# Layer 1's gate and branch products: weights as the moving operand, 512 features at a time

## The chip, the cores and the metric

The kernel runs on one core of a Trainium2 chip. The metric is device time in microseconds (us) of one execution; lower is better.

## What is computed

The reference is a backbone of two layers over 256 latent tokens and, in layer 0 only, 256 context tokens (layer 1 uses the context for its keys and values alone). The part of a layer that matters here, cut to it:

```
p       = rmsnorm(x) modulated  @ w_in                      # 256 x 1024 times 1024 x 6400
gates   = sigmoid(p[..., 9*256:])                            # 4 gates of 1024 features
branches = (retention, short conv, fourier, pooling)         # each 256 tokens x 256 features
merged  = sum over i of gates[i*1024:(i+1)*1024] * (branches[i] @ w_branch[i])
mix     = merged @ w_o
x       = x + g1 * rmsnorm(mix);  then the feed-forward half of the layer
```

## The kernel before

All activations are kept turned: features on the 128 partitions, tokens along the row. Layer 0 has 512 tokens in a row (latents and context), layer 1 has 256 latent tokens for most of its work.

Every float32 product is made of three matmuls of fp32r parts (`mm3`, L220): hi x hi, hi x lo and lo x hi. A weight block comes from memory by one DMA on SP's queue (`raw`), ACT makes its hi part (L102) and DVE its lo part (L112). `Weights` (L48 to L140) does this ahead of use: blocks are split two steps before the step that uses them, into a ring of four; a block of exactly 1024 columns with an odd number uses a second pair of raw buffers (L77), a block of 1280 columns does not. So blocks of 1280 columns share two raw buffers, blocks of 1024 columns have four.

The program is a list of steps written out in order. After each step, `tick` (L228) advances up to two of the waiting "sides" by one stage: small pieces of other work (the retention's stages, the Fourier branch, the pooling's end, the norms and turns of the context chain of the layer before) that are put on the engines' queues between two steps. A `yield` in such a piece is the point where it pauses until a later tick. So one `yield` puts one step of matmuls between two stages.

In layer 1 the gates are computed by `gate` (L1060), once for each of 8 feature tiles m and 4 branches i: `proj` (L708) takes a 128x128 weight tile as the stationary operand and 256 tokens of `h` as the moving one, 8 tiles deep, so 24 matmuls of 256 columns (tile `gate`); then 6 matmuls of 256 columns give the branch product (tile `pb`). ACT makes the sigmoid (`sg`), DVE multiplies and adds into `mg` (L1072 to L1075). `merge` (L1091) splits a finished `mg` into hi and lo for `wo` (L1184), the product with w_o, which has `merged` as the stationary operand and 512 weight columns as the moving one.

The order of layer 1: Fourier and conv projections; four gate blocks of branch 1 (`NFILL`, L1099), between which the context chain of layer 0 is turned by PE transposes (tile `xt`, L558, into banks of the group "b") and modulated by DVE and ACT (`hf`, `hf0hi`, `hf0lo`, L472); v, then k, q and g of both head pairs, the pooling projections; then the other 28 gate blocks, into which the retention's stages (L797: `ktp`, `st`, `sc`, `y`, `var`, `yr`, once for each head pair c) are put by the ticks; then `wo`.

PSUM has eight banks. "a" has four (0 to 3), "b" three (4 to 6), "m" one; `bank` (L183) hands out a group's banks in turn.

Of the kernel before, what the change touches and what calls it, by code (L numbers as in the profile page):

```python
# [8 lines left out]
F32 = mybir.dt.float32  # L9
# [8 lines left out]
P = 128  # L18
D = 1024
# [146 lines left out]
def kernel(ctx: ExitStack, tc: tile.TileContext, a: dict, out: bass.AP):  # L166
# [3 lines left out]
    def pool(name, bufs=1, stack=ctx, **kw):  # L170
        return stack.enter_context(tc.tile_pool(name=name, bufs=bufs, reuse_waits="tile", **kw))
# [11 lines left out]
    def bank(tag, name, shape=None, keep=False):  # L183

        i = banks[tag].pop(0)
        if not keep:
            banks[tag].append(i)
        t = psum.tile([P, 512], F32, tag=f"bank{i}", name=name)
        return t if shape is None else cut(t, shape)
# [38 lines left out]
    def tick(n=2):  # L228

        for g in sides[:n]:  # L230
            sides.remove(g)
            if next(g, "end") != "end":
                sides.append(g)
# [365 lines left out]

        return do  # L600

    def tail(steps, bl, fn, nt, chains, eager, before=None, ahead=2, keep=KEEP):

        do = doer(steps)
        m = keep - 2
        n = len(bl) - keep
        lead = 2 if before else 0
        for k, b in enumerate(bl[:lead]):  # L610
            steps.append(Step([b], partial(fn, b, k, (0, 1)), free=[], tick=False))
            do(partial(before, k))
        for k, b in enumerate(bl[:lead]):
            steps.append(Step([], partial(fn, b, k, (2, 3)), free=[b], tick=False))
            do(partial(before, lead + k))
        for k, b in enumerate(bl[:n]):
            if k < lead:
                continue
            steps.append(Step([b], partial(fn, b, k, range(nt)), tick=False))
            if before and k + lead < n:  # L620
                do(partial(before, k + lead))
        if before:
            do(*[partial(before, k) for k in range(n, len(bl))])
        passes = [(0,), (1,)] + [(2, 3)] * (nt == 4)
        for ts in passes:
            final = ts == passes[-1]
            for j, b in enumerate(bl[n:]):

                hs = [(b, 0), (b, 1)] if len(ts) > 1 or j < m else [(bl[-2], j - m), (bl[-1], j - m)]
                for t in ts:  # L630
                    run = [partial(fn, x, bl.index(x), (t,), (half,)) for x, half in hs]
                    st = Step(([b] if len(ts) > 1 or j < m else bl[-2:]) if t == 0 else [], lambda run=run: [f() for f in run], tick=t > 0)
                    st.free = [b] if t == nt - 1 and (len(ts) > 1 or j < m) else bl[-2:] if t == nt - 1 and j == keep - 1 else []
                    st.ahead, st.lag = ahead if final else 2, final and nt == 2
                    if st.lag:
                        st.ahead = 1
                    steps.append(st)
            c = chains[ts[0] // 2]
            if final and nt == 2:
                do(drain_sides, partial(c.one, 1), partial(c.three, 0))  # L640
                steps[-1].lag, steps[-1].ahead = True, 1
                do(partial(c.two, 1), partial(c.three, 1))
                steps[-1].lag = True
            elif nt == 2:
                do(lambda c=c: sides.append(staged([partial(c.one, 0), partial(c.two, 0)])))
            elif final and eager:
                todo = c.norms(ts)
                do(*todo[:2])

                do(*todo[2:-1], flush, todo[-1])  # L650
                steps[-1].ahead, steps[-1].lag = ahead + 1, True
            else:
                todo = c.norms(ts) + (c.turns() if ts[-1] % 2 else [])
                do(lambda todo=todo: sides.append(staged(todo)))
# [4 lines left out]
    def mixer(l, h, hnext, start=None):  # L659
# [22 lines left out]

        def begin():
            bp = pool(f"br{l}", stack=outer)
            P_["m"] = pool(f"mg{l}", 2 if l == 0 else 4, stack=outer)
            P_["t"] = pool(f"rt{l}", stack=early)
            P_["o"] = pool(f"op{l}", 5 if l == 0 else 4, stack=early)
            for i in range(NBR):
                br.append([[bp.tile([P, T], F32R, name=f"br{l}{i}{c}{x}") for c in range(2)] for x in range(2)])
            t = P_["t"]  # L690
            vt.extend(rt(f"v{s}", [2, HEADS, DH], f"v{l}{s}") for s in range(2))
            fix["kt"] = rt("kt", [2, MIX], f"kt{l}")
            fix["pw"] = t.tile([P, 2, P], F32, name=f"pw{l}")
            nc.vector.memset(fix["pw"], 0.0)
# [102 lines left out]
        def retention(c):  # L797
# [14 lines left out]
            for t in range(2):  # L812
                for d in range(2):
# [4 lines left out]
                        op=ALU.mult,  # L818
                    )
            yield  # L820
            pst = bank("a", f"st{l}{c}", [2 * DH])
            for t in range(2):
                for j in range(2):
# [28 lines left out]
            def heads(s, am):  # L852
                sl = slice(s * SEQ, (s + 1) * SEQ)
                py = bank("a", f"y{l}{c}{s}")[:, :SEQ]
                n = 4 if s == 0 else 2
                for i in range(n):
                    for j in range(2):
                        if i < 2:
                            lhs, rhs = vt[s][:, i, 2 * c + j, :], am[j][:, i, :]
                        else:  # L860
                            lhs, rhs = st[off[j], (i - 2) * DH : (i - 1) * DH], qd[off[j], i - 2, :]
                        nc.tensor.matmul(py[off[j], :], lhsT=lhs, rhs=rhs, start=(i == 0), stop=(i == n - 1))
                ys = rt("ys", [2, SEQ], "ys", 2)
                nc.scalar.activation(ys[:, 0, :], py, AF.Square)
                nc.vector.tensor_tensor(ys[:, 1, :], py, gs[:, sl], op=ALU.mult)
                return ys
# [26 lines left out]
            for s in range(NS - 1, -1, -1):  # L893
                am[s] = scores(s)
                yield
                am[s] = heads(s, am[s])
                yield
            rx = {s: variance(s, am[s]) for s in am}
            yield
            for s in am:  # L900
                normed(s, am[s], rx[s])

# [155 lines left out]
        acc = {}  # L1058

        def gate(blk, m, i):  # L1060
            while i == 2 and not {0, 1} <= set(made) or i == 0 and "ret" not in made:
                tick()
            ps = proj(blk, f"gate{l}{m}{i}")
            sg = P_["m"].tile([P, T], F32, tag="sg", name="sg", bufs=2)
            nc.scalar.activation(sg, ps, AF.Sigmoid)  # L1065
            pb = bank("b", f"pb{l}{m}{i}")[:, :T]
            for c in range(2):
                sl = slice(1024 + c * P, 1024 + (c + 1) * P)
                mm3(pb, (blk.hi[:, sl], blk.lo[:, sl]), (br[i][0][c], br[i][1][c]), c == 0, c == 1)
            if m not in mg:  # L1070
                mg[m] = P_["m"].tile([P, T], F32, tag="mg", name="mg")
                nc.vector.tensor_tensor(mg[m], sg, pb, op=ALU.mult)  # L1072
            else:
                nc.vector.tensor_tensor(sg, sg, pb, op=ALU.mult)
                nc.vector.tensor_tensor(mg[m], mg[m], sg, op=ALU.add)  # L1075
# [17 lines left out]
            split(*parts, mg.pop(m))  # L1093
            merged[m] = parts

        lead = 2 if l == 0 else 4
        GATES = [(m, i) for i in (1, 2, 3, 0) for m in range(lead)]
        GATES += [(m, i) for m in range(lead, KC) for i in (1, 2, 3, 0)]
        NFILL = 4  # L1099
        seen = {}  # L1100

        def gate_steps(todo):
            for m, i in todo:
                b = Block(a["w_gate"][l, m, i], f"gt{l}{m}{i}", 1280)
                steps.append(Step([b], lambda b=b, m=m, i=i: gate(b, m, i)))
                seen[m] = seen.get(m, 0) + 1
                if seen[m] == NBR:
                    if m == 0:
                        do(close_early)
                    do(at(merge, m))  # L1110
# [57 lines left out]
        else:  # L1168
# [3 lines left out]
                add(fourier, FU + c, c)  # L1172
            for c in range(2):
                conv_steps(c)
            gate_steps(GATES[:NFILL])
            do(drain_sides, lambda: set_tag("b"))
            add_many(lambda b: [v_step(b, s) for s in range(2)], v_blocks())
            qkg_steps(0)
# [12 lines left out]

        chains = [Chain(l, 0, s, acc, "ab"[s], hnext) for s in range(NS)]

        gate_steps(GATES[NFILL if l else 0 :])
        do(*[c.load for c in chains])
        bl = [Block(a["w_o"][l, m], f"wo{l}{m}") for m in range(KC)]
        tail(steps, bl, wo, NT, chains, True, ahead=AH[l], keep=KEEPS[l])

        def close():
            late.close()  # L1200
# [404 lines left out]
def _layouts(v):  # L1605
# [18 lines left out]
    d["w_q0"] = c(wq).reshape(2, P, 1024)  # L1624
    wg = d["w_in"][:, GATE:].reshape(DEPTH, NBR, KC, P, 1024).transpose(0, 2, 1, 3, 4)
    wb = v["w_branch"].reshape(DEPTH, NBR, 2, P, KC, P).transpose(0, 4, 1, 3, 2, 5)
    d["w_gate"] = np.concatenate([wg, wb.reshape(DEPTH, KC, NBR, P, 2 * P)], 4)
    d["w_in"] = c(d["w_in"][:, :GATE])
    d["w_o"] = c(v["w_o"]).reshape(DEPTH, KC, P, D)
    wu = v["ffn_w_up"].reshape(DEPTH, KC, P, 2 * NF, P).transpose(0, 3, 2, 1, 4)  # L1630
# [65 lines left out]
```

## Time and profile before

| | us |
|---|---|
| median of 3 runs (1219.34 to 1221.39) | 1221.35 |
| the profiled execution, its own time | 1220.89 |
| its span, first to last instruction | 1219.1 |
| PE busy (matmuls) | 1189.1 |
| PE weight loads busy | 1028.8 |
| DVE busy | 783.1 |
| ACT busy | 453.2 |
| mean granted TensorE clock | 0.995 |

The duration that the profile gives a matmul is longer than the distance at which matmuls follow each other, since one begins while the one before is still in the pipeline. Where PE runs without a pause, the distance between two starts is what one costs.

### The profile page before, as it was taken

The numbers are of one execution on the slowest core, as the hardware profiler recorded it, in microseconds if no ns is written. First come the engines' busy times: TensorE is split into PE (matmuls) and PEld (weight loads), VectorE is DVE, ScalarE is ACT, GpSimd is POOL, SyncE is SP. The second block draws the span as 40 slices with busy tenths as digits, with TensorE's granted clock in tenths as the row PEclk, the third lists the DMA queues.
The fourth block names the chain that finished last, engine by engine and source line by source line (L and its number), as shares of the span: only waits on it lengthen the run. The fifth ranks groups of instructions, "written<-read, shape, count | busy, mean of one in ns | idle before, by whom it ended". The sixth has DMA issues, their size and how long they took to land.

```text
span 1219.1 us, 17611 instructions
## 1 busy us (share of the span) xinstructions
PE 1189.1 (98%) x6960; PEld 1028.8 (84%) x6960; DVE 783.1 (64%) x1275; ACT 453.2 (37%) x715; POOL 41.7 (3%) x39
## 2 busy tenths in 40 slices
PE   7999999999999989999999999989989999999997
PEld 5987778888888878888888888889879998999986
DVE  5464745586875656775777673576666666666644
ACT  4332323323222643222322222564334445444442
POOL 1500000000000100000000000000000000000000
PEclk9999999999999999999999999999999999999999
DMA  8642325457565225666666773334455663665662
GB/s 290 233 131 70 112 87 190 150 180 172 183 194 161 67 104 170 210 204 169 233 204 215 245 234 97 130 111 160 125 155 163 199 233 112 191 183 181 201 214 86
DMA packets 66435, 205.67 MB, mean 169 GB/s; under 512 B 14640, under 2 KB 18480, under 8 KB 66352
## 3 DMA queue, kind: packets, MB, share of 16 engines
q1 hardware_dynamic: 65776, 204.39, 53.6%
q8 instruction: 55, 0.90, 0.3%
q14 instruction: 28, 0.23, 0.1%
q10 hardware_dynamic: 576, 0.16, 0.1%
HBM read 203.41 MB, written 1.11 MB: 168 GB/s over the span
## 4 chain that ended last, share of the span: by engine, by line
PE 87%; DVE 5%; ACT 4%; DMA 2%; issue 2%; POOL 1%; SPq 0%; DVEq 0%; POOLq 0%; ACTq 0%
PE up L223 10%; PE up L224 10%; PE up L222 10%; PE gate L222 7%; PE gate L224 7%; PE gate L223 7%; PE dn L224 4%; PE dn L223 4%; PE dn L222 4%; PE pb L224 2%; PE pb L223 2%; PE pb L222 2%; PE wo L224 1%; ACT junk L443 1%; PE wo L223 1%
## 5 line engine op out<-in xcount | busy, mean ns | idle before, releaser
L338 DVE SCALAR_TENSOR_TENSOR mjunk<-raw_mod,crow 128x1024 bf16<-128x1024 f32 x128 | 156.4, 1222 | 8.8 <-DMA raw_mod<-in_w_modt 6.8
L223 PE MATMUL up<-hm0lo,hi_up 128*128 128x512 f32 (+1 forms) x384 | 143.5, 374 | 2.8 <-DVE hm0lo L470 2.8
L224 PE MATMUL up<-hm0hi,lo_up 128*128 128x512 f32 (+1 forms) x384 | 143.2, 373 | 2.5 <-DVE lo_up L112 2.5
L222 PE MATMUL up<-hm0hi,hi_up 128*128 128x512 f32 (+1 forms) x384 | 143.5, 374 | 0.0
L112 DVE TENSOR_TENSOR lo_up<-raw_up,hi_up 128x1024 fp32r<-128x1024 f32 x88 | 107.6, 1223 | 36.6 <-ACT hi_up L102 36.5
L112 DVE TENSOR_TENSOR lo_gt<-raw_gt,hi_gt 128x1280 fp32r<-128x1280 f32 x64 | 95.3, 1489 | 31.4 <-ACT hi_gt L102 31.4
L222 PE MATMUL gate<-h0hi,hi_gt 128*128 128x512 f32 x256 | 100.6, 393 | 0.0
L222 PE MATMUL up<-hm1hi,hi_up 128*128 128x256 f32 x352 | 99.8, 284 | 0.0
L223 PE MATMUL up<-hm1lo,hi_up 128*128 128x256 f32 x352 | 99.7, 283 | 0.1
L223 PE MATMUL gate<-h0lo,hi_gt 128*128 128x512 f32 x256 | 99.6, 389 | 0.0
L224 PE MATMUL gate<-h0hi,lo_gt 128*128 128x512 f32 x256 | 99.6, 389 | 0.0
L224 PE MATMUL up<-hm1hi,lo_up 128*128 128x256 f32 x352 | 99.6, 283 | 0.0
L102 ACT ACTIVATE hi_up<-raw_up 128x1024 fp32r<-128x1024 f32 x88 | 92.2, 1049 | 9.5 <-DMA raw_up<-in_w_up 8.9
L102 ACT ACTIVATE hi_gt<-raw_gt 128x1280 fp32r<-128x1280 f32 x64 | 81.0, 1265 | 21.1 <-DMA raw_gt<-in_w_gate 21.0
L112 DVE TENSOR_TENSOR lo_dn<-raw_dn,hi_dn 128x1024 fp32r<-128x1024 f32 x44 | 53.6, 1224 | 54.1 <-ACT hi_dn L102 54.1
L223 PEld LDWEIGHTS up<-hm0lo,hi_up 128*128 128x128 f32 x384 | 72.8, 190 | 16.0 <-DVE hm0lo L470 3.7
L224 PEld LDWEIGHTS up<-hm0hi,lo_up 128*128 128x128 f32 x384 | 72.9, 190 | 15.3 <-DVE lo_up L112 2.7
L1065 ACT ACTIVATE sg<-gate 128x512 f32<-128x512 f32 (+1 forms) x64 | 31.3, 488 | 143.6 <-PE gate L224 143.5
L222 PEld LDWEIGHTS up<-hm0hi,hi_up 128*128 128x128 f32 x384 | 72.9, 190 | 12.5
L102 ACT ACTIVATE hi_dn<-raw_dn 128x1024 fp32r<-128x1024 f32 x44 | 46.4, 1058 | 91.8 <-PE dn L224 68.3
L222 PE MATMUL gate<-hf0hi,hi_gt 128*128 128x256 f32 x256 | 73.5, 287 | 0.0
L223 PE MATMUL gate<-hf0lo,hi_gt 128*128 128x256 f32 x256 | 72.4, 283 | 0.0
(342 smaller groups left out, 2718.3 us busy)
## 6 DMA issues: line engine op xcount, KB each, us to landing
raw_up<-in_w_up SPq DMA_DIRECT2D x88, 512.0 KB, 3.9
raw_gt<-in_w_gate SPq DMA_DIRECT2D x64, 640.0 KB, 3.9
raw_mod<-in_w_modt SPq DMA_DIRECT2D x80, 512.0 KB, 4.1
raw_dn<-in_w_down SPq DMA_DIRECT2D x44, 512.0 KB, 4.3
raw_in<-in_w_in SPq DMA_DIRECT2D x28, 512.0 KB, 3.7
raw_wo<-in_w_o SPq DMA_DIRECT2D x16, 512.0 KB, 4.1
raw_mod<-in_w_mod SPq DMA_DIRECT2D x12, 512.0 KB, 5.2
grow<-gscr SPq DMA_DIRECT2D x6, 512.0 KB, 7.2
```

The costliest lines, as they stand in the source:

```text
L102: self.nc.scalar.activation(b.hi, b.raw, AF.Copy)
L112: self.nc.vector.tensor_tensor(b.lo, b.raw, b.hi.bitcast(F32), op=ALU.subtract)
L222: nc.tensor.matmul(ps, lhsT=st[0], rhs=mv[0], start=first, stop=False)
L223: nc.tensor.matmul(ps, lhsT=st[0], rhs=mv[1], start=False, stop=False)
L224: nc.tensor.matmul(ps, lhsT=st[1], rhs=mv[0], start=False, stop=last)
L338: nc.vector.scalar_tensor_tensor(junk, b.raw, 1.0, crow[s], op0=ALU.mult, op1=ALU.mult, accum_out=out()[:, s, i : i + 1])
L443: nc.scalar.activation(junk, src, AF.Square, scale=1.0 / 32.0, accum_out=acc)
L1065: nc.scalar.activation(sg, ps, AF.Sigmoid)
```

## The change

In layer 1 the gates and branch products are computed the other way round: 128 tokens of `h` (or of a branch) are stationary, 512 weight columns move, and the result has tokens on the partitions and 512 features in a row. A unit is one half g of the features and one branch i: four blocks of 1024 columns with the gate's weights (two k tiles of 512 features each), then one with the branch's. The two token tiles t accumulate side by side in two kept banks of "b". The products are merged by rows, `merge_wide` turns them back by PE transposes (tile `mt`) and splits them from PSUM. Layer 1 takes bank 7 into "b". In the retention, three more pauses stand in each pass for layer 1. Layer 0 keeps its code; its instructions keep their order.

```diff
         def begin():
-            P_["m"] = pool(f"mg{l}", 2 if l == 0 else 4, stack=outer)
+            P_["m"] = pool(f"mg{l}", 2, stack=outer)
+            if l:
+                banks["b"] += [banks["m"].pop()]
...
             yield
+            if l:
+                yield
             pst = bank("a", f"st{l}{c}", [2 * DH])
...
                 am[s] = scores(s)
                 yield
+                if l:
+                    yield
                 am[s] = heads(s, am[s])
                 yield
             rx = {s: variance(s, am[s]) for s in am}
             yield
+            if l:
+                yield
             for s in am:
                 normed(s, am[s], rx[s])
...
         def gate(blk, m, i):
-            while i == 2 and not {0, 1} <= set(made) or i == 0 and "ret" not in made:
-                tick()
...
+        wide, gts, mgs = 512, {}, {}
+        def gate_wide(blk, g, i, kp):
+            for t in range(NT):
+                if kp == 0:
+                    gts[t, "i"] = banks["b"][0]
+                    gts[t] = bank("b", f"gate{l}{g}{i}{t}", keep=True)
+                ts = slice(t * P, (t + 1) * P)
+                for j in range(2):
+                    k, sl = 2 * kp + j, slice(j * wide, (j + 1) * wide)
+                    mm3(gts[t], [x[k][:, ts] for x in h], (blk.hi[:, sl], blk.lo[:, sl]), k == 0, k == KC - 1)
+                if kp == 3:
+                    sg = gts[t, "s"] = P_["m"].tile([P, wide], F32, tag="sg", name="sg")
+                    nc.scalar.activation(sg, gts[t], AF.Sigmoid)
+                    banks["b"].append(gts[t, "i"])
+        def branch_wide(blk, g, i):
+            while i == 2 and not {0, 1} <= set(made) or i == 0 and "ret" not in made:
+                tick()
+            for t in range(NT):
+                pb = bank("b", f"pb{l}{g}{i}{t}")
+                ts = slice(t * P, (t + 1) * P)
+                for c in range(2):
+                    sl = slice(c * wide, (c + 1) * wide)
+                    mm3(pb, [x[c][:, ts] for x in br[i]], (blk.hi[:, sl], blk.lo[:, sl]), c == 0, c == 1)
+                sg = gts.pop((t, "s"))
...
+                    nc.vector.tensor_tensor(sg, sg, pb, op=ALU.mult)
+                    nc.vector.tensor_tensor(mgs[g, t], mgs[g, t], sg, op=ALU.add)
+        def merge_wide(g, half):
+            pt = bank("b", f"mt{l}{g}{half}", [2, T])
+            for j in range(2):
+                for t in range(NT):
+                    src = mgs[g, t][:, (2 * half + j) * P : (2 * half + j + 1) * P]
+                    nc.tensor.transpose(pt[:, j, t * P : (t + 1) * P], src, ident)
...
+                split(*merged[m], pt[:, j, :])
+        ORDER = [(g, i) for g in range(2) for i in (1, 2, 3, 0)]
...
+                    if (g, i) == (1, 1) and kp in (1, 2):
+                        do(at(merge_wide, 0, kp - 1))
...
-        NFILL = 4
+        NFILL = 1
...
-            gate_steps(GATES[:NFILL])
+            wide_steps(ORDER[:NFILL])
...
-        gate_steps(GATES[NFILL if l else 0 :])
+        if l:
+            wide_steps(ORDER[NFILL:])
+        else:
+            gate_steps(GATES)
...
+        mids = {1: at(merge_wide, 1, 0), 2: at(merge_wide, 1, 1)} if l else {}
+        tail(steps, bl, wo, NT, chains, True, ahead=AH[l], keep=KEEPS[l], mids=mids)
```

`tail` runs `mids[k]` behind the k-th block of w_o. The weights of layer 1's gates are laid out anew in memory (`w_gate1`: 40 blocks of 512 KB in place of 32 of 640 KB).

Three places show how the instructions move.

PE, where the context chain is turned between the gate products ahead of v. Names: `gate`, `pb` and `xt` are PSUM tiles, `hf0hi`/`hf0lo` the parts of h, `hi_gt`/`lo_gt` the parts of a gate block. Before:

```order
L222 MATMUL pb_7085<-br_6643,hi_gt_6962 128x256
L223 MATMUL pb_7085<-br_6645,hi_gt_6962 128x256
L224 MATMUL pb_7085<-br_6643,lo_gt_6963 128x256
L222 MATMUL pb_7085<-br_6644,hi_gt_6962 128x256
L223 MATMUL pb_7085<-br_6646,hi_gt_6962 128x256
L224 MATMUL pb_7085<-br_6644,lo_gt_6963 128x256
L565 MATMUL xt_7094<-ident,prod_6710 128x128
L565 MATMUL xt_7094<-ident,prod_6760 128x128
L565 MATMUL xt_7097<-ident,prod_6710 128x128
L565 MATMUL xt_7097<-ident,prod_6760 128x128
```

And now:

```order
L222 MATMUL gate_7067<-hi_gt_6966,hf0hi_6529 128x512
L223 MATMUL gate_7067<-lo_gt_6967,hf0hi_6529 128x512
L224 MATMUL gate_7067<-hi_gt_6966,hf0lo_6537 128x512
L222 MATMUL gate_7067<-hi_gt_6966,hf0hi_6530 128x512
L223 MATMUL gate_7067<-lo_gt_6967,hf0hi_6530 128x512
L224 MATMUL gate_7067<-hi_gt_6966,hf0lo_6538 128x512
L565 MATMUL xt_7074<-ident,prod_6710 128x128
L565 MATMUL xt_7074<-ident,prod_6760 128x128
L565 MATMUL xt_7077<-ident,prod_6710 128x128
L565 MATMUL xt_7077<-ident,prod_6760 128x128
```

Between two turns there stood 30 matmuls of 256 columns; now there stand 12 of 512, and two banks of "b" stay with the gates over all of it.

ACT, in the second pass of the retention (head pair 1), from the copy `kt` of the turned keys to the copy `st` of the state that PE's `st` matmuls make. Before:

```order
L810 ACTIVATE kt_6657<-ktp_7808 128x2x128
L102 ACTIVATE hi_gt_7817<-raw_gt_7704 128x1280
L1065 ACTIVATE sg<-gate_7823 128x256
L997 ACTIVATE pmf<-pm_7859,chan 128x256
L211 ACTIVATE br_6652<-pmf 128x256
L833 ACTIVATE st<-st_7865 128x128
```

And now:

```order
L814 ACTIVATE kt_6657<-ktp_7788 128x2x128
L102 ACTIVATE hi_gt_7797<-raw_gt_7685 128x1024
L102 ACTIVATE hi_gt_7821<-raw_gt_7713 128x1024
L839 ACTIVATE st<-st_7841 128x128
L102 ACTIVATE hi_gt_7849<-raw_gt_7737 128x1024
L102 ACTIVATE hi_gt_7877<-raw_gt_7761 128x1024
```

One block was split (one step) between the two stages; now it is two blocks, two steps, and the pooling's end (`pmf`, `br`) no longer lies between them.

PE, inside `wo`, where the second half of the features is turned:

```order
L223 MATMUL wo_8525<-lo_wo_8485,mh_8121 128x512
L224 MATMUL wo_8525<-hi_wo_8484,ml_8122 128x512
L1144 MATMUL mt_8550<-ident,mg 128x128 x4
L222 MATMUL wo_8516<-hi_wo_8510,mh_8148 128x512
L223 MATMUL wo_8516<-lo_wo_8511,mh_8148 128x512
```

Four transposes stand behind the second block of w_o, four more behind the third; before, `wo` ran without anything between its blocks. The other eight `mt` transposes stand between gate matmuls.

## Rows read from the trace of the kernel before

**Rows 1.** The page, busy time of each engine (us, share of the span, instructions).
```profile
PE 1189.1 (98%) x6960; PEld 1028.8 (84%) x6960; DVE 783.1 (64%) x1275; ACT 453.2 (37%) x715; POOL 41.7 (3%) x39
```
**Rows 2.** Windows: length, busy us (x) of PE, PEld, DVE, ACT, POOL; clock, DMA share, GB/s.
```profile
784.00:838.00 54.00, 50.61 (x383) 48.12 (x382) 39.12 (x81) 34.52 (x71) 2.40 (x4) 0.97 0.45 146
838.00:885.00 47.00, 45.48 (x331) 41.01 (x331) 29.16 (x58) 15.93 (x26) 1.02 (x1) 1.00 0.41 125
...
920.00:996.00 76.00, 76.00 (x632) 75.83 (x632) 49.49 (x69) 35.82 (x49) 0.00 (x0) 1.00 0.60 194
```
**Rows 3.** Groups by form, 784 to 1012: busy us, mean ns | idle before.
```profile
L222 PE MATMUL gate<-hf0hi,hi_gt 128*128 128x256 f32 x256 | 73.5, 287 | 0.0
```
**Rows 4.** Timeline of PE, layer 1's gates: start, duration; 24 matmuls apart.
```profile
930.25 0.28 PE L222 MATMUL gate<-hf0hi,hi_gt 128*128 128x256 f32 x1
...
933.13 0.28 PE L222 MATMUL pb<-br,hi_gt 128*128 128x256 f32 x1
```
**Rows 5.** Timeline of PE, layer 1's wo, 49 matmuls apart.
```profile
1000.74 0.39 PE L223 MATMUL wo<-lo_wo,mh 128*128 128x512 f32 x1
...
1011.85 0.39 PE L224 MATMUL wo<-hi_wo,ml 128*128 128x512 f32 x1
```
**Rows 6.** Timeline of PE, the gates ahead of v and the turns between them.
```profile
820.94 0.55 PE L565 MATMUL xt<-ident,prod 128*128 128x128 f32 x3 [0.88 <-ACT prod L554]
...
829.80 0.29 PE L224 MATMUL pb<-br,lo_gt 128*128 128x256 f32 x1
829.93 0.60 PE L565 MATMUL xt<-ident,prod 128*128 128x128 f32 x4
830.28 0.36 PE L222 MATMUL gate<-hf0hi,hi_gt 128*128 128x256 f32 x1
...
838.18 0.28 PE L222 MATMUL vps<-hi_v,hf0hi 128*128 128x256 f32 x1
```
**Rows 7.** Waits of PE from 780 to 1040: us in total, times, longest.
```profile
PE st L825 <- ACT br L211: 1.1, 1, 1.1
PE yr L885 <- DVE rx L878: 0.9, 1, 0.9
PE y L862 <- DVE am L848: 0.9, 1, 0.9
...
PE vps L223 <- DVE lo_v L112: 0.6, 1, 0.6
PE pb L222 <- DVE mg L1072: 0.2, 1, 0.2
PE pb L222 <- ACT sg L1065: 0.2, 1, 0.2
```
**Rows 8.** Timeline of DVE, from the first to the second turn.
```profile
824.73 0.54 DVE L483 TENSOR_SCALAR hf<-xt,am,sh 128x256 f32<-128x256 f32 x1
...
828.97 0.54 DVE L483 TENSOR_SCALAR hf<-xt,am,sh 128x256 f32<-128x256 f32 x1
```
**Rows 9.** Timeline of ACT, the same stretch: the two hi parts of a turn.
```profile
825.31 0.72 ACT L487 ACTIVATE hf0hi<-hf 128x256 fp32r<-128x256 f32 x2 [0.49 <-DVE hf L483]
```
**Rows 10.** Groups by form, 784 to 1012: splits of blocks of 1024 and 1280 columns.
```profile
L112 DVE TENSOR_TENSOR lo_gt<-raw_gt,hi_gt 128x1280 fp32r<-128x1280 f32 x32 | 47.7, 1491 | 21.6 <-ACT hi_gt L102 21.6
L102 ACT ACTIVATE hi_gt<-raw_gt 128x1280 fp32r<-128x1280 f32 x32 | 40.5, 1265 | 17.1 <-DMA raw_gt<-in_w_gate 17.0
L112 DVE TENSOR_TENSOR lo_in<-raw_in,hi_in 128x1024 fp32r<-128x1024 f32 x16 | 19.5, 1222 | 3.9 <-ACT hi_in L102 3.7
...
L102 ACT ACTIVATE hi_in<-raw_in 128x1024 fp32r<-128x1024 f32 x15 | 15.7, 1050 | 8.0 <-PE vps L224 8.0
```
**Rows 11.** Timeline of DVE, second pass of the retention: its table comes late.
```profile
901.76 0.69 DVE L834 TENSOR_TENSOR qd<-qd,q 128x512 f32<-128x512 f32 x1 [3.94 <-DMA qd<-vscr]
```
**Rows 12.** Windows, two stretches around the conv's last product.
```profile
814.00:816.00 2.00, 0.76 (x3) 0.56 (x4) 1.50 (x3) 2.00 (x5) 0.34 (x1) 0.83 0.00 0
816.00:818.00 2.00, 2.00 (x10) 2.00 (x11) 1.48 (x3) 1.06 (x1) 0.00 (x0) 0.50 0.00 0
```

More of the change, by code (lines that the diff above doesn't have):

```diff
@@ L600, in doer, with tail @@
         return do
-    def tail(steps, bl, fn, nt, chains, eager, before=None, ahead=2, keep=KEEP):
+    def tail(steps, bl, fn, nt, chains, eager, before=None, ahead=2, keep=KEEP, mids={}):
         do = doer(steps)
@@ L621, in tail @@
                 do(partial(before, k + lead))
+            if k in mids:
+                do(mids[k])
         if before:
@@ L1094, in merge @@
             merged[m] = parts
-        lead = 2 if l == 0 else 4
+        wide, gts, mgs = 512, {}, {}
[12 more added lines that the diff above has]
+                    banks["b"].append(gts[t, "i"])
@@ new lines, in branch_wide @@
+        def branch_wide(blk, g, i):
[8 more added lines that the diff above has]
+                sg = gts.pop((t, "s"))
+                if (g, t) not in mgs:
+                    mgs[g, t] = P_["m"].tile([P, wide], F32, tag="mg", name="mg")
+                    nc.vector.tensor_tensor(mgs[g, t], sg, pb, op=ALU.mult)
+                else:
+                    nc.vector.tensor_tensor(sg, sg, pb, op=ALU.mult)
+                    nc.vector.tensor_tensor(mgs[g, t], mgs[g, t], sg, op=ALU.add)
@@ new lines, in merge_wide @@
+        def merge_wide(g, half):
[4 more added lines that the diff above has]
+                    nc.tensor.transpose(pt[:, j, t * P : (t + 1) * P], src, ident)
+            for j in range(2):
+                m = 4 * g + 2 * half + j
+                merged[m] = [P_["l"].tile([P, T], F32R, name=f"m{x}{l}{m}") for x in ("h", "l")]
+                split(*merged[m], pt[:, j, :])
@@ new lines, in mixer, with wide_steps @@
+        ORDER = [(g, i) for g in range(2) for i in (1, 2, 3, 0)]
+        def wide_steps(todo):
+            for g, i in todo:
+                for kp in range(5):
+                    b = Block(a["w_gate1"][g, i, kp], f"gt{l}{g}{i}{kp}")
+                    if kp < 4:
+                        steps.append(Step([b], lambda b=b, g=g, i=i, kp=kp: gate_wide(b, g, i, kp)))
+                    else:
+                        steps.append(Step([b], lambda b=b, g=g, i=i: branch_wide(b, g, i)))
+                    if (g, i) == (1, 1) and kp in (1, 2):
+                        do(at(merge_wide, 0, kp - 1))
+                if (g, i) == (0, 0):
+                    do(close_early)
@@ L1097, in mixer @@
+        lead = 2
         GATES = [(m, i) for i in (1, 2, 3, 0) for m in range(lead)]
         GATES += [(m, i) for m in range(lead, KC) for i in (1, 2, 3, 0)]
-        NFILL = 4
+        NFILL = 1
         seen = {}
@@ L1103, in gate_steps @@
             for m, i in todo:
-                b = Block(a["w_gate"][l, m, i], f"gt{l}{m}{i}", 1280)
+                b = Block(a["w_gate"][m, i], f"gt{l}{m}{i}", 1280)
                 steps.append(Step([b], lambda b=b, m=m, i=i: gate(b, m, i)))
@@ L1192, in mixer @@
         chains = [Chain(l, 0, s, acc, "ab"[s], hnext) for s in range(NS)]
-        gate_steps(GATES[NFILL if l else 0 :])
+        if l:
+            wide_steps(ORDER[NFILL:])
+        else:
+            gate_steps(GATES)
         do(*[c.load for c in chains])
         bl = [Block(a["w_o"][l, m], f"wo{l}{m}") for m in range(KC)]
-        tail(steps, bl, wo, NT, chains, True, ahead=AH[l], keep=KEEPS[l])
+        mids = {1: at(merge_wide, 1, 0), 2: at(merge_wide, 1, 1)} if l else {}
+        tail(steps, bl, wo, NT, chains, True, ahead=AH[l], keep=KEEPS[l], mids=mids)
         def close():
@@ L1626, in _layouts @@
     wb = v["w_branch"].reshape(DEPTH, NBR, 2, P, KC, P).transpose(0, 4, 1, 3, 2, 5)
-    d["w_gate"] = np.concatenate([wg, wb.reshape(DEPTH, KC, NBR, P, 2 * P)], 4)
+    d["w_gate"] = np.concatenate([wg, wb.reshape(DEPTH, KC, NBR, P, 2 * P)], 4)[0]
+    w1 = np.stack([v["w_in"][1][:, GATE * P :].reshape(D, NBR, 2, 512)[:, i] for i in range(NBR)])
+    w1 = np.concatenate([w1, v["w_branch"][1].reshape(NBR, 2 * P, 2, 512)], 1).reshape(NBR, 5, 2, P, 2, 512)
+    d["w_gate1"] = c(w1.transpose(4, 0, 1, 3, 2, 5)).reshape(2, NBR, 5, P, 1024)
     d["w_in"] = c(d["w_in"][:, :GATE])
```

## The prediction

> **What bounds the kernel now.** The page comes first: PE is busy for 98% of the span, DVE for 64%, ACT for 37% [rows 1]. That is a reason to look at PE, not yet a price, because the busy time counts the pipelined length of a matmul. So I went to the windows of the stretch that changes, layer 1's mixer [rows 2]. From 920 to 996, where only gate and branch products run, PE has no pause, DVE is busy 49.5 of 76 us, ACT 35.8, the DMA engines 60% of the time at 194 GB/s: PE alone sets the pace there, and a matmul saved is time saved. From 784 to 838 PE misses 3.4 of 54 us and the clock is below full, from 838 to 885 it misses 1.5: there waits count too. The list of PE's waits names them [rows 7], and for the price of one matmul I read distances between starts in the timeline.
>
> **The price of a matmul.** In the gates, 24 matmuls of 256 columns lie between 930.25 and 933.13 [rows 4]: 2.88/24 = 0.120 us each, although each is listed with 0.28. In `wo`, which has the very form that the change gives the gates (128 activations stationary, 512 weight columns moving), 49 lie between 1000.74 and 1011.85 [rows 5]: 11.11/49 = 0.2267 us. Doubling the columns costs 0.107 us more, so 0.013 us of a matmul does not depend on its columns, and joining two saves 2 x 0.120 - 0.2267 = 0.0133 us. That is the whole gain in streaming: the columns are the same in number.
>
> The Trainium skill, page "TensorE: Matmul & The Clock Gate", section "Back-to-back issue gap", speaks against it: a matmul alone takes N/2.4 + 2.5 ns, so joining two would save 2.5 ns. The rows show 13 ns instead; by the page the first term of the sum would be about 1 us, and the time 1218.0.
>
> **The change, part by part.**
>
> *Gates and branch products.* Before: 32 blocks of 24 + 6 matmuls x 3.60 us (30 x 0.120). The 24 are there in the groups: 256 matmuls on each of three lines, so 768 [rows 3]. Now 8 units of 60 matmuls of 512 columns, 13.60 us each. The first unit stands in the fill ahead of v, where other things pace PE, and is costed below. The other 28 blocks took 100.8 us, the 7 units take 95.2: **-5.6 us**. I give it 0.3 us either way, for the reading of the starts.
>
> *The turn back.* New: 16 PE transposes in four groups of four. The nearest row is a group of four `xt` transposes between matmuls: the last `pb` starts at 829.80, the next gate matmul at 830.28, so 0.36 us lie behind `pb`'s own 0.12, and that gate matmul is 0.08 longer than usual [rows 6]. 4 x 0.44 = **+1.8 us**; between 0.36 and 0.6 us a group: +1.4 to +2.4. What the transposes wait for is long done: the first two groups stand 5.4 us of gate matmuls behind the last branch product of half 0, the other two behind two blocks of w_o, also 5.4 us; DVE has two products, two sums and a split of 1.2 us [rows 10] to do in it, under 4 us. The split of the turned rows has two blocks of w_o before `wo` wants it. I cost it at nothing; if that cover fails, it costs 1 to 2 us once.
>
> *ACT and DVE.* A split of 1024 columns takes 1.05 and 1.22 us, of 1280 columns 1.27 and 1.49 [rows 10]; 40 of the former take 1.6 us more on ACT and 1.2 more on DVE than 32 of the latter, while products, sums and sigmoids halve in number. A block lasts 2.72 us on PE. Both engines stay under PE: nothing. The DMAs bring the same bytes, and blocks of 1024 columns get four raw buffers in place of two, so they are asked for earlier. At a pace 5.9% higher, 194 GB/s becomes 205 and the DMA share 0.60 becomes 0.64 [rows 2]: nothing.
>
> *More steps in the retention.* Four of PE's waits belong to it: `st` 1.1 us, `yr` 0.9, `y` 0.9 and `pb` for a sigmoid 0.2 [rows 7]. All four waited for work of one or two us on ACT or DVE that was given one step, 3.6 us, behind a queue of splits. Now there are two steps, 5.4 us, in each of these places, and the raw block whose lateness held the queue ahead of `am` is asked for earlier. I take them all off: **-3.1 us**; from 0 to -3.1, since each can come back elsewhere. What is moved with the stages: the four table loads of a pass stand in SP's queue between weight loads, and DVE's `qd` waited 3.94 us for them [rows 11] with the next split queued behind it. It can do so again; the block behind it is wanted by PE two steps later, some 5 us, so it holds. No stage falls out at the end: 18 stages in place of 12 are over before the branch product that needs the retention.
>
> *The fill ahead of v.* Here the turns of the context chain stand between the gate products. The two kept gate banks leave two of "b"'s four for the turns, and a turn uses both; so each turn waits until DVE and ACT have read the one before. Their loop per turn is `hf` 0.54, two `hf0hi` 0.72, hi split 1.05, lo split 1.22 [rows 8 to 10]: 3.53 us, while PE has 12 matmuls and a turn, 2.72 + 0.44 = 3.16. In the kernel before the loop is there too: 4.24 us from `hf` to `hf` [rows 8] against 30 x 0.120 + 0.44 = 4.04 on PE. So each turn waits about 0.4 us, the first about 0.9 (its `hf` ended at 825.27 [rows 8], now about 0.9 earlier, since two pairs of shorter splits lie ahead; PE, which turned from 820.5 on, is through the first block at 823.5); the branch product waits 0.4 for the same bank. Five blocks 13.6, turns 0.3 + 3 x 0.44, waits 2.1: 17.3 us, against 17.24 from 820.94 to 838.18 [rows 6]. The wait of 0.88 before it [rows 6] shrinks by 0.48, because the `prod` it waits for stands behind one hi and one lo split on ACT and DVE. **-0.4 us** in all; if the waits vanish -2.5, if they double +1.7.
>
> *v.* Its wait of 0.6 for `lo_v` [rows 7] stays: nothing. If the fill ends later, it goes.
>
> **The sum.** -5.6 + 1.8 - 3.1 - 0.4 = -7.3 us on the profiled execution's 1220.89 us (span 1219.1, 1.8 around it): **1213.5 us**. That execution is 0.5 us below the median of the runs. The ends: -5.9 + 1.4 - 3.1 - 2.5 = -10.1 and -5.3 + 2.4 + 0 + 1.7 = -1.2, so 1210.8 to 1219.7.
>
> **Rivals.**
>
> 1. *The waits in the retention move instead of going.* The late tables hold DVE, the splits behind it come late, and PE waits for those. For it: DVE ended two of these waits, and the 3.94 us are its own. Against: more buffers, two steps of slack. The gain of 3.1 is lost: 1216.7 us. Chance 0.20.
> 2. *More goes than I count.* The fill's turns fit under the gate products, and v's wait goes: 2.1 + 0.6 less: 1210.8 us. For it: the loop and PE's work differ by only 0.4 us. Chance 0.12.
> 3. *Joining saves nothing.* If a matmul cost its columns alone once the activations are stationary, 420 joined pairs would save none of the 5.6 us: 1219.1 us. This is the direction in which the page quoted above points. Against: `wo` has this form and carries the same 0.013 us [rows 5]. Chance 0.04.
> 4. *Slower: the fill's waits take the clock down.* The clock was granted at half (1.2 of 2.4 GHz) from 816 to 818, after PE had been busy for 0.76 of the 2 us before, and only 10 matmuls started in 2 us, 0.2 us each in place of 0.12 [rows 12]. If the turns' waits kept it there for the whole fill, 60 matmuls would take about 0.43 instead of 0.23 us: +12 us, 1225.5 us. It decides if the turns leave PE as idle as it was then; I expect waits of 0.4 us between stretches of 3.2 us of work. The Trainium skill, same page, section "The HAM clock gate", says that idleness throttles and activity releases; rows 12 agree with the first half. Chance 0.05.
> 5. *A wait that I cannot place*, in the kept banks or the new turn, eats the gain: about 1221 us. Chance 0.04. That the change does not do what it says is no case of its own: the order on PE and ACT shows the wide matmuls and the two steps.
>
> **How the numbers follow.** The forecast has 0.55. No change is what a measurement cannot tell from it, within 0.2%, 2.4 us of 1221.35: above 1218.9 and below 1223.8. Faster are the forecast and rivals 1 and 2, less the part of rival 1 where the fill's waits double as well: 0.86. Same are that part, rival 3 and half of 5: 0.08. Slower are rival 4 and the rest: 0.06. The range from 1210.0 to 1218.5 takes in rivals 1 and 2 and the lower end of the sum; it leaves out rivals 3 to 5 and the worst end, some 0.15.
>
> **What would show it.** Starts of gate matmuls 0.227 us apart; a unit of 60 in 13.6 us; `mt` groups costing 0.44 us; no wait of `st`, `yr` and `y`; waits of `xt` of 0.3 to 0.9 us in the fill, and v starting near where it did, 0.4 us earlier; from the first turn to the end of `wo` 7 us less. It is wrong if the distance is not 0.227, if new waits of several us stand in front of `pb`, `mt` or `y`, or if the granted clock is below full between 821 and 838.

## The result and the profile after

| us | before | changed |
|---|---|---|
| median (4 runs each) | 1220.34 (1219.17 to 1221.39) | 1212.45 (1209.47 to 1212.90) |
| profiled execution, span | 1220.89, 1219.1 | 1212.68, 1210.9 |

The ratio is 0.993, 95% interval 0.9917 to 0.9943: 7.9 us faster by the medians, 8.2 by the two profiled executions. The forecast was 7.3 less, 1213.5 us (1220.89 - 7.3 is 1213.6). The page of the changed kernel gives its busy times [rows 1]:

```profile
PE 1183.7 (98%) x6495; PEld 1004.5 (83%) x6496; DVE 779.4 (64%) x1255; ACT 451.6 (37%) x707; POOL 41.3 (3%) x39
```

PE has 465 matmuls fewer, but its busy time falls by only 5.4 us and its share stays at 98%, so these do not give the gain. Where the time went is read from the stretches between the first matmuls of the same work in both timelines of PE:

| stretch on PE's timeline (us) | before | changed | difference |
|---|---|---|---|
| all ahead of layer 1's first product `fu` (code unchanged) | 790.51 | 790.91 | +0.40 |
| `fu` to the first gate | 30.73 | 30.26 | -0.47 |
| first gate to v (the fill) | 16.94 | 16.78 | -0.16 |
| v to k | 12.38 | 12.03 | -0.35 |
| k to the second group of gates | 34.69 | 32.93 | -1.76 |
| second group of gates to `wo` | 109.80 | 103.00 | -6.80 |
| `wo` to the feed-forward's first product | 29.80 | 30.74 | +0.94 |
| from there to the end | 194.25 | 194.25 | 0 |

The sum is -8.20, the difference of the two spans. Code that is the same in all these kernels does not take the same time in every execution: over the eleven profiled runs the part ahead of `fu` takes 787.8 to 791.7 us, the last part 194.2 to 195.7, while the stretches between repeat within 0.02 in the one kernel that was profiled twice. So the +0.40 lies within chance, layer 1 itself gained 8.60, and in what follows the price of a part is read from the stretches.

Most of it lies between the second group of gates and `wo`. In PE's timeline (start, duration, engine, line, operation, out<-in, shapes; in brackets, where there is any, the idle time before it), first before, with two of the retention's waits, then changed:

```profile
884.76 0.41 PE L885 MATMUL yr<-ident,rx 128*128 128x128 f32 x2 [0.91 <-DVE rx L878]
...
885.25 0.47 PE L222 MATMUL gate<-hf0hi,hi_gt 128*128 128x256 f32 x1
...
905.30 1.68 PE L862 MATMUL y<-am,v 128*64 128x256 f32 x8 [0.88 <-DVE am L848]
...
995.05 0.40 PE L222 MATMUL wo<-hi_wo,mh 128*128 128x512 f32 x1
```

```profile
882.91 0.58 PE L222 MATMUL gate<-hi_gt,hf0hi 128*128 128x512 f32 x1
...
911.35 1.08 PE L868 MATMUL y<-am,v 128*64 128x256 f32 x8
...
945.11 0.39 PE L222 MATMUL gate<-hi_gt,hf0hi 128*128 128x512 f32 x1
...
985.91 0.39 PE L222 MATMUL wo<-hi_wo,mh 128*128 128x512 f32 x1
```

The windows of the changed kernel (columns as in [rows 2]) show the same from the other side: in the second, PE now misses 0.2 us of 47 where it missed 1.5, and the gates run without a pause.

```profile
784.00:838.00 54.00, 50.80 (x327) 45.04 (x325) 39.48 (x81) 35.48 (x72) 2.39 (x4) 0.97 0.46 144
838.00:885.00 47.00, 46.78 (x334) 42.21 (x333) 31.43 (x61) 15.43 (x26) 0.00 (x0) 1.00 0.52 151
...
920.00:988.00 68.00, 68.00 (x307) 56.25 (x306) 42.96 (x49) 32.84 (x40) 0.00 (x0) 1.00 0.59 188
```

PE's waits from 780 to 1040, all that the list has (before: [rows 7]):

```profile
PE xt L565 <- DVE prod L556: 2.2, 2, 1.8
PE bg L222 <- ACT hi_in L102: 1.5, 1, 1.5
PE bg L224 <- DVE lo_in L112: 0.8, 1, 0.8
PE xt L565 <- DVE hf L483: 0.6, 1, 0.6
PE vps L223 <- DVE lo_v L112: 0.2, 1, 0.2
PE xt L565 <- ACT prod L554: 0.2, 1, 0.2
```

The four waits of the retention (`st`, `yr`, `y`, `pb`) are gone and none stands in their place. New is `hf`, 0.6 us, the first turn in the fill. In PE's timeline a wide gate matmul follows the one before at (921.92 - 919.65)/10 = 0.227 us, the distance of `wo` in [rows 5]; over the 180 from 945.11 to 985.91, with nothing between them, it is 0.2267:

```profile
919.65 0.39 PE L223 MATMUL gate<-lo_gt,hf0hi 128*128 128x512 f32 x1
...
921.92 0.39 PE L224 MATMUL gate<-hi_gt,hf0lo 128*128 128x512 f32 x1
...
935.79 0.39 PE L224 MATMUL gate<-hi_gt,hf0lo 128*128 128x512 f32 x1
936.02 0.60 PE L1144 MATMUL mt<-ident,mg 128*128 128x128 f32 x4
936.38 0.47 PE L222 MATMUL gate<-hi_gt,hf0hi 128*128 128x512 f32 x1
936.69 0.39 PE L223 MATMUL gate<-lo_gt,hf0hi 128*128 128x512 f32 x1
```

Four `mt` transposes move the gates from 936.02 to 936.38 and the next matmul by another 0.08: 0.44 us, as `xt` did in [rows 6]. In the fill DVE's `hf` (before: [rows 8]) now comes every 3.42 us; behind it, the second table of the retention, which had cost DVE 3.94 us [rows 11]:

```profile
824.18 0.54 DVE L483 TENSOR_SCALAR hf<-xt,am,sh 128x256 f32<-128x256 f32 x1
827.60 0.54 DVE L483 TENSOR_SCALAR hf<-xt,am,sh 128x256 f32<-128x256 f32 x1
...
903.31 0.69 DVE L840 TENSOR_TENSOR qd<-qd,q 128x512 f32<-128x512 f32 x1 [0.99 <-DMA qd<-vscr]
```

### The profile page after: what moved, and what is told of

It reads as the page before. It is cut to its first block, busy times and chain, and to the rows that moved or that the text cites. A ratio compares the mean times of both kernels' runs of the same rounds, so it can differ in the third digit from the quotient of the medians.

```text
span 1210.9 us, 16622 instructions
## 1 busy us (share of the span) xinstructions
PE 1183.7 (98%) x6495; PEld 1004.5 (83%) x6496; DVE 779.4 (64%) x1255; ACT 451.6 (37%) x707; POOL 41.3 (3%) x39
## 4 chain that ended last, share of the span: by engine, by line
PE 89%; DVE 4%; ACT 4%; issue 1%; DMA 1%; POOL 0%; SPq 0%; POOLq 0%; DVEq 0%; ACTq 0%
PE up L223 10%; PE up L224 10%; PE up L222 10%; PE gate L222 7%; PE gate L224 7%; PE gate L223 7%; PE dn L224 5%; PE dn L223 5%; PE dn L222 4%; PE pb L222 2%; PE pb L224 2%; PE pb L223 2%; PE wo L224 1%; ACT junk L443 1%; PE wo L223 1%
## 5 line engine op out<-in xcount | busy, mean ns | idle before, releaser
L112 DVE TENSOR_TENSOR lo_gt<-raw_gt,hi_gt 128x1024 fp32r<-128x1024 f32 (+1 forms) x72 | 95.7, 1339 | 31.5 <-ACT hi_gt L102 31.5
L102 ACT ACTIVATE hi_gt<-raw_gt 128x1024 fp32r<-128x1024 f32 (+1 forms) x72 | 81.7, 1147 | 16.0 <-PE gate L224 8.2
L223 PE MATMUL dn<-lo_dn,shi 128*128 128x512 f32 x176 | 68.6, 390 | 0.0
L222 PE MATMUL dn<-hi_dn,shi 128*128 128x512 f32 x176 | 68.5, 389 | 0.0
L224 PE MATMUL dn<-hi_dn,slo 128*128 128x512 f32 x176 | 68.5, 389 | 0.0
```

Of the source, the lines that this page charges most:

```text
L102: self.nc.scalar.activation(b.hi, b.raw, AF.Copy)
L112: self.nc.vector.tensor_tensor(b.lo, b.raw, b.hi.bitcast(F32), op=ALU.subtract)
L222: nc.tensor.matmul(ps, lhsT=st[0], rhs=mv[0], start=first, stop=False)
L223: nc.tensor.matmul(ps, lhsT=st[0], rhs=mv[1], start=False, stop=False)
L224: nc.tensor.matmul(ps, lhsT=st[1], rhs=mv[0], start=False, stop=last)
```

## The experiments

Each is timed against the kernel before on the same chip. The ratios are to it, with 95% intervals; "stretch" means those of the table above.

**The change again**, as the mark for the other runs.

> The changed kernel as it is, as the mark for the runs beside it. Every theory expects the time that it had, near 1212.5 us, 0.993 of the kernel before.

1212.16 us against 1221.01, ratio 0.9923 (0.9911 to 0.9935). From `fu` to the end the stretches agree with the first profile within 0.02 us; ahead of `fu`, in the unchanged code, this execution is 3.0 us shorter.

**Without the added pauses.** From the changed kernel:

```diff
-            if l:
-                yield
             pst = bank("a", f"st{l}{c}", [2 * DH])
...
                 yield
-                if l:
-                    yield
                 am[s] = heads(s, am[s])
...
-            if l:
-                yield
             for s in am:
                 normed(s, am[s], rx[s])
```

> The changed kernel with the retention's pauses of before (one step between the stages, now of 2.7 us where it was 3.6). Theory: the second step is what took PE's waits at st, yr and y away, so they come back: 3 us more than the changed kernel (2 to 5), with waits of 0.5 to 2 us each at st, y and yr. Rival: the earlier weight loads (four raw buffers) and the other order did it, and the steps are worth nothing: within 0.5 us of the changed kernel.

1218.40 us, ratio 0.9977 (0.9968 to 0.9986): 6.2 us slower than with them, more than I had expected. PE's waits in this kernel:

```profile
PE st L829 <- DVE vd L818: 1.8, 1, 1.8
PE yr L889 <- DVE rx L882: 1.7, 2, 0.9
PE y L866 <- DVE am L852: 1.7, 1, 1.7
```

They stand at the three places of [rows 7] again, but are 5.2 us in all where they had been 2.9. `st` now waits for DVE's `vd`, not for ACT's `br`, and `yr` waits in both passes. The stretch from k to the gates gives back 1.76, that from the gates to `wo` 4.32. The reason is the step: the same work of ACT and DVE now has one gate step of 2.72 us to hide behind, not one of 3.60, 0.88 less. In the timelines `y` waits 1.69 us for 0.88 before, `yr` of the second pass 0.79 for none, both some 0.8 more; `yr` of the first pass, which stands behind a step of the pooling projections that did not change, waits 0.91 as before. So the pauses do not only remove 3.1 us of old waits; they also pay for the shorter step.

**Two raw buffers for layer 1's gate blocks**, as before the change:

```diff
-            if b.at > last and b.n == 1024 and i % 2:
+            if b.at > last and b.n == 1024 and i % 2 and not b.name.startswith("gt1"):
```

> The changed kernel with two raw buffers for layer 1's gate blocks, as blocks of 1280 columns had. Theory: with two steps in each place the queue holds out, 0 to 0.7 us more. Rival: the earlier loads are what freed DVE's queue; then waits at y or pb come back as in the kernel before, 1.5 to 3 us more.

1220.06 us, ratio 0.9989 (0.9981 to 0.9997): 7.9 us slower than with four, nearly the whole gain, and more than any of the theories gave. The stretch from the gates to `wo` is 8.6 us longer. The group of hi splits on ACT, 784 to 1004, first with four buffers, then with two:

```profile
L102 ACT ACTIVATE hi_gt<-raw_gt 128x1024 fp32r<-128x1024 f32 x40 | 41.2, 1053 | 12.7 <-PE gate L224 8.2 <-DMA raw_gt<-in_w_gate 2.9 <-PE pb L224 1.3
```

```profile
L102 ACT ACTIVATE hi_gt<-raw_gt 128x1024 fp32r<-128x1024 f32 x40 | 42.2, 1057 | 51.5 <-DMA raw_gt<-in_w_gate 49.5 <-DVE sg L1135 1.9
```

With two, ACT sits idle for 49.5 us until weights land, though the bytes are the same. In its timeline (two splits, five blocks apart), and in the list of DMA issues from 850 to 990 (KB each, median us to landing):

```profile
907.36 1.06 ACT L102 ACTIVATE hi_gt<-raw_gt 128x1024 fp32r<-128x1024 f32 x1 [5.44 <-DMA raw_gt<-in_w_gate]
...
922.04 1.06 ACT L102 ACTIVATE hi_gt<-raw_gt 128x1024 fp32r<-128x1024 f32 x1 [1.80 <-DMA raw_gt<-in_w_gate]
```

```profile
raw_gt<-in_w_gate SPq DMA_DIRECT2D x35, 512.0 KB, 3.5
```

The five blocks take 14.68 us, 2.94 each, where PE needs 2.72. It is a loop: a buffer is loaded (3.5), read for hi (1.06) and for lo (1.22), and only then loaded again: 5.8 us, so 2.9 a block with two buffers. In the kernel before the same loop takes 3.8 (the median of its gate loads from 920 to 996) + 1.27 + 1.49 [rows 10] = 6.6 us for two blocks of 1280 columns, which is less than PE's 7.2. The change shortened PE's step by more than it shortened the loop.

PE's list of waits has only 3.2 us of this:

```profile
PE gate L223 <- DVE lo_gt L112: 2.8, 5, 0.8
...
PE pb L223 <- DVE lo_gt L112: 0.4, 2, 0.2
```

Most of the rest is in PE's timeline and carries no wait:

```profile
935.25 0.39 PE L222 MATMUL gate<-hi_gt,hf0hi 128*128 128x512 f32 x1
935.65 0.50 PE L223 MATMUL gate<-lo_gt,hf0hi 128*128 128x512 f32 x1
935.98 0.39 PE L224 MATMUL gate<-hi_gt,hf0lo 128*128 128x512 f32 x1
```

The second starts 0.40 after the first, not 0.23, and the third 0.33 after the second. A stall shorter than the part of a matmul that overlaps the next (0.39 listed less 0.23 of distance, 0.16) leaves no idle time, yet here it costs 0.17 + 0.10. From 925 to 994 such excesses of distance between gate and branch matmuls add to 6.7 us over 33 places, and the list of waits has 2.5 us of them; in the changed kernel to 0.2, all of it behind `mt`.

**Wide products in halves.** Each matmul of 512 columns is written as two of 256, but for the first of each sum:

```diff
+            for c in (slice(0, 256), slice(256, 512)):
+                nc.tensor.matmul(ps[:, c], lhsT=st[i], rhs=mv[j][:, c], start=False, stop=last and n == 2 and c.start > 0)
```

> The changed kernel with each wide matmul of layer 1's gates and branch products (but for the first of each sum) made as two of 256 columns: 448 matmuls more, the same columns. Theory: a matmul costs 0.0133 us beyond its columns, so 448 x 0.0133 = 6.0 us more (5 to 7), and starts 0.120 us apart. Rival: the two halves have the same stationary operand behind each other and the fixed part is paid only for a new one, or joining saves nothing: 0 to 1 us more.

1217.08 us, ratio 0.9968 (0.9956 to 0.9981), 4.9 us slower than whole. The stretch from the gates to `wo` is 4.63 longer by 392 more matmuls, 0.0118 us each. In its timeline (x2: two in one row) 12 matmuls take 926.66 - 925.22 = 1.44 us, 0.120 each, as when the tokens moved [rows 4]:

```profile
925.22 0.40 PE L233 MATMUL gate<-hi_gt,hf0hi 128*128 128x256 f32 x2
...
926.66 0.40 PE L233 MATMUL gate<-hi_gt,hf0hi 128*128 128x256 f32 x2
```

So the gain in streaming is the fixed part of a matmul, whichever operand moves. Each half has a weight load of its own (the page counts 6944, against 6496 for the whole), so this run does not tell a price of the load from one of the matmul, and the rival of a fixed part for new operands only is not tested by it. The other 56 added matmuls stand in the fill, where they cost nothing in sum (+0.1 there, -0.1 in v), since the loop of DVE and ACT sets the pace; I had counted them with the rest (448 x 0.0133 = 6.0).

**The pauses alone, in the kernel before** (the three `yield` of the change, nothing else):

```diff
             yield
+            if l:
+                yield
             pst = bank("a", f"st{l}{c}", [2 * DH])
...
```

> The kernel before with the three more pauses in the retention and nothing else. Its 14 steps between the first retention stage and the first product that needs the retention don't hold 18 stages, so the last of them (y, var, yr) come behind each other. Theory: the waits at st and yr of the first pass go (about 2 us less), but the stages without a step between them make PE wait for ACT, DVE and POOL in turn, 4 to 7 us: 2 to 5 us slower than the kernel before. Rival: the pauses are worth 3 us by themselves, wherever they stand: 3 us faster.

1224.24 us against 1220.29, ratio 1.0029 (1.0017 to 1.0040): slower by 4.0 by the medians. Two things happen. The stretch from k to the gates is 1.76 us shorter, as in the change: the wait of `yr` in it goes (1.1 us with the overlap that it breaks), and `var` and `yr` themselves (0.7 us) now stand behind the first gates. But the 28 blocks of the old form are too few steps for 18 stages: when the branch product that needs the retention comes up, the last stages run one behind the other, with nothing between them. PE's timeline there:

```profile
917.34 1.08 PE L864 MATMUL y<-qd,st 64*64 64x256 f32 x8
919.88 0.61 PE L873 MATMUL var<-bsel,ys 128*128 128x2 f32 x4 [1.46 <-ACT ys L866]
923.05 0.66 PE L887 MATMUL yr<-ident,rx 128*128 128x128 f32 x2 [2.56 <-DVE rx L880]
923.36 0.56 PE L222 MATMUL gate<-hf0hi,hi_gt 128*128 128x256 f32 x1
```

and its windows (columns as in [rows 2]):

```profile
919.00:923.00 4.00, 0.61 (x4) 0.52 (x4) 2.19 (x4) 0.83 (x2) 1.01 (x1) 0.73 0.63 216
923.00:925.00 2.00, 1.95 (x10) 1.98 (x10) 0.77 (x2) 0.42 (x1) 0.00 (x0) 0.50 0.46 182
925.00:927.00 2.00, 2.00 (x11) 2.00 (x11) 0.07 (x1) 0.00 (x0) 0.00 (x0) 0.50 0.03 8
927.00:929.00 2.00, 2.00 (x16) 2.00 (x16) 0.00 (x0) 0.39 (x1) 0.00 (x0) 0.83 0.00 0
```

PE waits 4.0 us; then the granted clock is 0.50, half, until about 927.5, and the matmuls started from 923.36 to 927.56 follow each other at 0.21 us in place of 0.12: 1.8 us more. With the 0.7 us of `var` and `yr` that moved in, and without the old waits of `st`, `y` and `pb`, which went, the stretch from the gates to `wo` grew by 4.14. Both stretches together are 2.4 us longer; the 4.0 of the medians holds more than that, 0.9 us of it behind the mixer in the profiled execution, in code that is the same. The Trainium skill, page "TensorE: Matmul & The Clock Gate", section "The HAM clock gate", says that idleness throttles and activity releases; these rows agree with both halves. The wide form has 35 blocks in the place of these 28, and there `yr` is at 922.15 and the first branch product behind it at 927.86.

**Neither pauses nor buffers: the wide form alone** (the edits of the second and third experiment together):

> The changed kernel with two raw buffers for layer 1's gate blocks and the retention's pauses of before: the wide products alone. Both parts have been taken out one at a time (1218.4 and 1220.1 us, against 1212.2). Theory 1: the two losses are separate and add, 1226 us. Theory 2: late loads and short pauses hold PE in the same stretch, so the one hides in part behind the other: 1220 to 1223 us. In both the wide products alone are no gain over the kernel before (1221).

1226.37 us against 1221.29, ratio 1.0039 (1.0024 to 1.0055): the wide form by itself is slower than the kernel before. The four kernels as ratios:

| wide form with | old pauses | added pauses |
|---|---|---|
| two raw buffers | 1.0039 | 0.9989 |
| four raw buffers | 0.9977 | 0.9923 |

The pauses give 0.0050 and 0.0054, the buffers 0.0062 and 0.0066: within the intervals they add up, as theory 1 has it, and neither loss hides behind the other. By the stretches from k to `wo` the two cost 6.1 and 8.6 us alone and 15.9 together, 1.2 more than their sum. Its waits are those of both experiments:

```profile
PE gate L223 <- DVE lo_gt L112: 3.0, 6, 0.8
...
PE y L866 <- DVE am L852: 2.2, 1, 2.2
...
PE yr L889 <- DVE rx L882: 1.7, 2, 0.9
PE st L829 <- DVE vd L818: 1.7, 1, 1.7
```

**A third raw buffer in the kernel before**, for every third gate block of layer 1:

```diff
+            if b.name.startswith("gt1") and i % 3 == 2:
+                b.tag = "graw"
```

> The kernel before with a third raw buffer for layer 1's gate blocks of 1280 columns (one small constant tile moved to another pool to make room). Theory: at 3.6 us a block two buffers keep up, except around the second pass of the retention, where ACT waited 4.7 us for a load; the wait of 0.9 at y and a part of the 1.1 at st go: 0.5 to 2 us faster than the kernel before. Rival: buffers are worth 5 us and more by themselves, as the run with two of them suggests.

1220.68 us against 1221.29, ratio 0.9994 (0.9984 to 1.0004): not distinguishable from no change. The wait of `y` falls from 0.88 to 0.13, the stretch from the gates to `wo` is 0.76 shorter, `st` and `yr` stay at 1.1 and 0.9. So the late weight block did hold `y`, as I had read; the other two waits were not its doing.

**Each turn back twice**, `for j in [0, 1] * 2` in `merge_wide`:

> The changed kernel with each group of four mt transposes done twice into the same bank. Theory: a transpose in a row of them costs 0.09 us, and they wait for nothing: 16 x 0.09 = 1.4 us more (1.2 to 1.8). Rival: a group's price is its change of operands, and four more cost nothing: under 0.5 us more; or the bank is held longer and pb or the splits wait: over 3 us more.

1213.20 us, ratio 0.9939 (0.9926 to 0.9953). The stretches to and from `wo` are 0.87 and 0.85 longer: 1.72 for 16 transposes, 0.108 each. The medians differ by 1.0 us with overlapping intervals, so the price rests on the stretches.

**The first unit's gate banks from group "a"**, which leaves all of "b" to the turns of the fill:

```diff
+                tag = "a" if (g, i) == (0, 1) else "b"
...
-                    gts[t] = bank("b", f"gate{l}{g}{i}{t}", keep=True)
+                    gts[t] = bank(tag, f"gate{l}{g}{i}{t}", keep=True)
```

> The changed kernel with the fill's two kept gate banks taken from group a, so that the turns of the context chain have four banks of group b. Theory of banks: the waits of the turns (0.6 us and four of 0.2 to 0.3) are for the banks, and v starts 1 us earlier. Rival: the loop of ACT and DVE (3.4 us a turn) sets the pace, so PE's waits only move to v, which needs the splits behind the turns: no gain, v ends within 0.4 us of where it did.

1212.36 us, ratio 0.9932 (0.9918 to 0.9946): no gain over the change. The fill is 0.70 us shorter and v begins earlier, and v to k is 0.70 longer. The turns now stand 3.18 us apart, PE's own pace, not 3.42. The wait of `hf` is gone and these have come:

```profile
PE vps L223 <- DVE lo_v L112: 0.7, 2, 0.5
PE pb L223 <- DVE lo_gt L112: 0.4, 1, 0.4
```

So the banks did hold the turns, but ACT's and DVE's splits set when v can run; the banks decide only where PE waits for them.

No run beats the change. By the prices found, the feed-forward's 1056 up products of 256 columns could be joined in the same way for some 528 x 0.0118 = 6.2 us less the transposes that turn the result back (22 tiles of 128 merged features by two of tokens, 44 x 0.108 = 4.8). The 1.4 us left by this estimate are less than a measurement of this kernel can tell, and it was not tried.

## Why the prediction was right

*Streaming*, -5.6: 840 gate and branch matmuls of 0.120 us [rows 4] became 420 of 0.2267, **-5.6**. The distance of `wo` was the right price, and the halves confirm its fixed part: 0.0118 us from the stretch, 0.0133 in the forecast. The 2.5 ns that the Trainium skill ("TensorE: Matmul & The Clock Gate", "Back-to-back issue gap") gives for an isolated matmul do not carry over to this stream, where the fixed part is about five times that, and rival 3 falls with it: joining paid.

*The turn back*, +1.8: two groups of 0.44 ahead of `wo`, +0.88, and +0.94 behind, **+1.8**.

*The retention*, -3.1: from k to `wo` the time fell by 8.56; without streaming (-5.6) and turns (+0.88), **-3.8** is left, where the four waits were. The forecast took their idle time, 3.1. That is less than a wait costs: at `y` the eight matmuls behind the wait took 1.68 us where they now take 1.08, and a wait also breaks the overlap of two matmuls. Nor had all four one gate step of 3.6 us, as the forecast says: the first `yr` stood behind a step of the pooling projections. Rival 1, that they move, did not come: the table's wait shrank from 3.94 to 0.99 and two steps hold it.

*The fill*, -0.4: -0.16, and -0.47 in the stretch ahead of it. The loop was forecast at 3.53 us a turn and is 3.42; the first turn waits 0.6, not 0.9, and the later ones show none in the list, though the turns stand 3.42 apart where PE's own work is 3.16: 0.26 us a turn in stalls too short to leave idle time. *v*, 0: it took 0.35 less, its wait for `lo_v` falling from 0.6 to 0.2.

Each term is within 0.7 us of its measure, and the mechanism of each is the one forecast. The misses, at the retention, the fill and v, all go the same way, so layer 1 gained 8.6 us for 7.3; that the profiled execution shows 8.2 is the chance +0.40 ahead of it. The chances hold a slip: same and slower add to 0.07 each, not 0.08 and 0.06.

What failed is the reasoning of one step that came out right, "the DMAs bring the same bytes, and blocks of 1024 columns get four raw buffers in place of two, so they are asked for earlier ... nothing". The zero holds, but I argued it by GB/s and by busy shares, and did not name the price if the cover were gone, 7.9 us. With two buffers the DMA engines were busy 57% of the time from 925 to 994, DVE 37.8 and ACT 30.0 of 69 us, all far from full, and the loop through them was still slower than PE. The rival to name as slower was this one, the wide form without enough buffers, and not rival 4 in the fill: its mechanism showed in the run with the pauses alone, behind 4 us of idling, and cost 1.8 us; in the fill of the changed kernel, with no wait over 0.6, the granted clock is 1.00 from 821 to 838. Likewise "from 0 to -3.1" for the pauses put them against the old step. Within the new kernel they are worth 6.2, and in the old one they lose 4.0 by the medians, 2.4 by the stretches.

## What to carry to other kernels

Price a matmul by the distance of starts, at both widths, on the same chip: the part that does not depend on columns is what joining saves. When a change shortens the step of the engine that bounds, recount in steps whatever hides behind it: each load, split and free loop per buffer, and each latency that was given "one step". And look for stalls in distances between starts too, since those shorter than the overlap of two matmuls are in no list of waits.

## What was not expected of the hardware

- A stall of 0.17 us ahead of a matmul was followed by another 0.10 before the one after it, at nearly every place where `lo_gt` came late (the run with two raw buffers, 935.25 to 935.98).
- With four buffers a 512 KB load takes longer, a median of 4.4 us against 3.5 with two (lists of DMA issues, 850 to 980 and 850 to 990), and the kernel is 7.9 us faster. In the changed kernel:

```profile
raw_gt<-in_w_gate SPq DMA_DIRECT2D x35, 512.0 KB, 4.4
```

- The fall of the clock to half ahead of the fill [rows 12] is still there, two microseconds later: its granted clock is 0.50 from 818 to 820, behind a stretch from 814 to 816 in which PE was busy for 0.50 of 2 us.

```profile
814.00:816.00 2.00, 0.50 (x2) 0.30 (x2) 1.48 (x2) 2.00 (x4) 0.75 (x1) 1.00 0.00 0
...
818.00:820.00 2.00, 2.00 (x11) 2.00 (x11) 1.35 (x5) 1.04 (x3) 0.00 (x0) 0.50 0.69 225
```
